# The delta net's substitution on 128 partitions, four columns of a block in each

## The chip, the cores and the metric

The kernel runs on one core of a Trainium2 chip. The metric is the device time of one execution in microseconds (us). The core's engines take their instructions from queues of their own, each in order: TensorE (PE; PEld is its weight load), VectorE (DVE), ScalarE (ACT), GpSimd (POOL) and SyncE (SP), which issues nearly all DMAs of this kernel.

## The reference

One layer of a hybrid decoder on 512 tokens with a width of 2048: six heads of stick-breaking attention, four groups of a gated short convolution, six heads of a gated delta net, an output projection, an MLP with squared ReLU, and the norms. The change is in the delta net. It cuts the 512 tokens into chunks and solves a unit lower triangular system in each:

```python
m = jnp.where(strict, jnp.einsum('bhnid,bhnjd->bhnij', k_beta, k) * decay, 0.0)
eye = jnp.eye(C, dtype=f32)
t_mat = lax.linalg.triangular_solve(eye + m, jnp.broadcast_to(eye, m.shape),
                                    left_side=True, lower=True, unit_diagonal=True)
u = t_mat @ v_beta
w = t_mat @ (k_beta * jnp.exp(g)[..., None])
...
def step(state, xs):
    q_c, k_c, u_c, w_c, a_c, gl_c = xs
    v_new = u_c - w_c @ state
    o = q_c @ state + a_c @ v_new
    state = state * jnp.exp(gl_c)[..., None, None] + jnp.swapaxes(k_c, -1, -2) @ v_new
    return state, o
```

## The kernel before

All large products are made as three matmuls of fp32r halves (`mm3`, L109 to L111). A weight arrives as `raw` by a DMA that SP issues (L100), ACT rounds it to `whi` (L103), DVE makes the rest `wlo` (L104); both feed PE. `gemm` makes 48 such matmuls of 512 columns from four weight loads of 256 KB. There are four buffers each of `raw`, `whi` and `wlo`, and three PSUM banks for results.

The delta net takes chunks of 128 tokens, four per head (NB = 4). For each head `gdn_in` makes three projections, their convolutions, SiLU and norms (DVE and ACT), and from them `MT`, the strictly triangular matrices of the four chunks, 128 x (4 x 128) fp32. `gdn_base` inverts unit triangular matrices: first the four 32 x 32 blocks on the diagonal of each chunk, 16 blocks per head, by substitution on DVE; then the blocks off the diagonal by small matmuls (L452, L461, L471, L476, L482; PSUM tiles `b`), which put the inverse back into `MT`. `gdn_scan` runs the chunks of a head in order (PSUM tiles `s` and `o`). `sc_group` and `gdn_gate` are other products of the same stage, without a tie to the substitution; they are written between the heads' parts.

Before the change the substitution goes like this. SP writes `MT` whole to DRAM (`sm`, L424); four DMAs fetch the diagonal blocks, one for each group of 32 rows, so that each of 16 partitions holds one whole block of 32 x 32 (`Bq`, L426). `Yq` is cleared and given a diagonal of ones by POOL (L431, L432). For i = 31 to 1, DVE multiplies a column of the block with a row of `Yq` (L436, i x (32 - i) products on each partition) and subtracts that from `Yq` (L438). `Yq` goes to DRAM (`sy`, L440) and back by four DMAs (L443) into `Xc`, 32 rows by row group; DVE turns its 32 x 32 blocks into `X0` (L447), which L452 takes first. `Bq` and `Yq` have two halves for odd and even heads.

A planner lays out the order of each engine's instructions ahead of the run, with a cost model of its own (`TileContext(nc, schedule_with_timeline_sim=True)`). `base` and `scan` put the head's substitution and scan 2000 places ahead in its priorities, weight loads go 400 ahead. The program's order of the heads' parts is that of L654 to L680: gdn_in(0), base(0), gdn_in(1), scan(0), sc_group(0), base(1), gdn_in(2), and so on.

Of the kernel before, what the change touches and what calls it, by code (L numbers as in the profile page):

```python
# [11 lines left out]
F32 = mybir.dt.float32  # L12
F32R = mybir.dt.float32r
AF = mybir.ActivationFunctionType
ALU = mybir.AluOpType

P = 128
T = 512
NB = T // P
# [35 lines left out]
def trunk(ctx, tc, xT, wv1, wv2, wa, wo, wu, wd, vec, wf, out, dbg=None):  # L55
    nc = tc.nc
    V, S, G, PE = nc.vector, nc.scalar, nc.gpsimd, nc.tensor
# [9 lines left out]
    dr = ctx.enter_context(tc.tile_pool(name="dr", bufs=1, space=bass.MemoryType.DRAM))  # L67
# [9 lines left out]
    def xps(tag):  # L77
        pool, bufs = pool_of[tag]
        return pool.tile([P, 512], F32, name=tag, tag=tag, bufs=bufs)
# [8 lines left out]
    def tmp(n=512):  # L88
        return per.tile([P, n], F32, name="tmp", tag="tmp", bufs=4)

    def big():
        return big_pool.tile([P, 2, 512], F32R, name="big", tag="big", bufs=16, align_bytes=256)

    def f32t(shape, name):
        return per.tile(shape, F32, name=name)
# [26 lines left out]
    def gemm(src, acts):  # L122
        p = mmps()
        for c in range(KT // CHUNK_KT):
            gemm_chunk(p, src, acts, c)
        return p
# [27 lines left out]
    ident = f32t([P, P], "ident")  # L154
# [32 lines left out]
    for k in range(KT):  # L187
# [3 lines left out]
        a = big()  # L191
# [4 lines left out]
        for b in range(NB):  # L196
            s = slice(b * P, (b + 1) * P)
# [15 lines left out]
    p = xps("r")  # L213
# [3 lines left out]
    p = xps("r")  # L217
# [24 lines left out]
    for c in range(2):  # L242
        t = tmp()
# [35 lines left out]
    def ytile(i):  # L279
        return y_pool.tile([P, 512], F32, name="y", tag=f"y{i}", bufs=(10, 6)[i])  # L280
# [27 lines left out]
    p = xps("r")  # L308
# [20 lines left out]
    def gt(shape, name, tag=None, bufs=1, dt=F32):  # L329
        return gp.tile(shape, dt, name=name, tag=tag or name, bufs=bufs)  # L330

    q4 = lambda a: a.rearrange("p (b f) -> p b f", b=NB)
# [25 lines left out]
    heads, gb = {}, {}  # L358

    def gdn_in(h):  # L360
# [29 lines left out]
        for b in range(NB):  # L390
            S.activation(out=q4(dts)[:, b], in_=q4(dts)[:, b], func=AF.Copy, scale=be[:, b, h:h + 1])
        AT, MT = ytile(1), gt([P, 512], "MT", bufs=3)
        for c in range(2):
# [4 lines left out]
            s = slice(2 * c, 2 * c + 2)  # L398
            V.tensor_tensor(out=q4(MT)[:, s], in0=pv[:, :, 0], in1=q4(dts)[:, s], op=ALU.mult)
            V.tensor_tensor(out=q4(AT)[:, s], in0=pv[:, :, 1], in1=q4(dti)[:, s], op=ALU.mult)  # L400
        st.update(kq=kq, vtok=vtok, AT=AT, MT=MT)
        heads[h] = st
# [10 lines left out]
    def gdn_base(h):  # L413


        MT = heads[h]["MT"]
        if not gb:
            gb.update(Bq=gt([P, 32, 32], "Bq"), Yq=gt([P, 32, 32], "Yq"), tq=gt([P, 256], "tq"),
                      Xc=gt([P, 256], "Xc"))
            G.memset(gb["Xc"], 0.0)  # L420
        Bq, Yq, tq, Xc = (gb[n] for n in ("Bq", "Yq", "tq", "Xc"))
        p0 = 32 * (h % 2)
        sm = dr.tile([P, NB, P], F32, name="sm", tag="sm", bufs=2)
        nc.sync.dma_start(out=sm, in_=q4(MT))  # L424
        for s in range(NB):
            nc.sync.dma_start(  # L426
                out=Bq[p0 + 4 * s:p0 + 4 * s + 4],
                in_=sm[32 * s:32 * s + 32, :, 32 * s:32 * s + 32].rearrange("a k b -> k a b"))
        B, Y, t = Bq[p0:p0 + 16], Yq[p0:p0 + 16], tq[p0:p0 + 16]
        Yf = Y.rearrange("p a b -> p (a b)")  # L430
        G.memset(Yf, 0.0)  # L431
        G.memset(Yf[:, 0:1024:33], 1.0)  # L432
        for i in range(31, 0, -1):
            n = 32 - i
            tv = t[:, :i * n].rearrange("p (a b) -> p a b", a=i)
            V.tensor_tensor(out=tv, in0=B[:, 0:i, i:i + 1].broadcast_to([16, i, n]),  # L436
                            in1=Y[:, i:i + 1, i:32].broadcast_to([16, i, n]), op=ALU.mult)
            V.tensor_tensor(out=Y[:, 0:i, i:32], in0=Y[:, 0:i, i:32], in1=tv, op=ALU.subtract)  # L438
        sy = dr.tile([16, 32, 32], F32, name="sy", tag="sy", bufs=2)
        nc.sync.dma_start(out=sy, in_=Y)  # L440
        Xv = q4(Xc)
        for s in range(NB):
            nc.sync.dma_start(  # L443
                out=Xv[32 * s:32 * s + 32, :, 32 * (s % 2):32 * (s % 2) + 32],
                in_=sy[4 * s:4 * s + 4].rearrange("k a b -> a k b"))
        X0 = gt([P, 256], "X0")
        V.transpose(out=X0, in_=Xc)  # L447
        p = xps("b")
        pv = q4(p[:, :128])
        for b in range(NB):  # L450
            for s in (0, 64):
                PE.matmul(pv[s + 32:s + 64, b], lhsT=q4(MT)[s:s + 32, b, s + 32:s + 64],  # L452
                          rhs=q4(X0)[s:s + 32, b, 0:32], start=True, stop=True)
        A1 = gt([P, 128], "A1")
        S.copy(out=A1[32:64], in_=p[32:64, :128])
        V.tensor_copy(out=A1[96:128], in_=p[96:128, :128])
        p = xps("b")
        pv = q4(p[:, :128])
        for b in range(NB):
            for s in (32, 96):  # L460
                PE.matmul(pv[s - 32:s, b], lhsT=q4(A1)[s:s + 32, b], rhs=Xv[s:s + 32, b, 32:64], start=True, stop=True)  # L461
        for s in (0, 2):
            r = slice(32 * s, 32 * s + 32)
            if s:
                V.tensor_scalar(out=Xv[r, :, 32:64], in0=pv[r], scalar1=-1.0, scalar2=None, op0=ALU.mult)
            else:
                S.mul(out=Xv[r, :, 32:64], in_=pv[r], mul=-1.0)
        lo, hi = slice(0, 64), slice(64, P)
        p = xps("b")
        for b in range(NB):  # L470
            PE.transpose(p[lo, b * 64:b * 64 + 64], Xc[lo, b * 64:b * 64 + 64], ident[lo, lo])  # L471
        X1 = gt([P, 256], "X1")
        S.copy(out=X1[lo], in_=p[lo, :256])
        p = xps("b")
        for b in range(NB):
            PE.matmul(q4(p[:, :256])[hi, b], lhsT=q4(MT)[lo, b, hi], rhs=q4(X1)[lo, b], start=True, stop=True)  # L476
        S.copy(out=X1[hi], in_=p[hi, :256])
        for r in (lo, hi):
            V.tensor_copy(out=q4(MT)[r, :, r], in_=Xv[r])
        p = xps("b")  # L480
        for b in range(NB):
            PE.matmul(q4(p[:, :256])[lo, b], lhsT=q4(X1)[hi, b], rhs=Xv[hi, b], start=True, stop=True)  # L482
        S.mul(out=q4(MT)[lo, :, hi], in_=q4(p[:, :256])[lo], mul=-1.0)
# [161 lines left out]
    def base(h):  # L645
        with tc.high_priority(CPRIO):
            gdn_base(h)
# [72 lines left out]
    for k in ORDER:  # L720
        a = big()
# [46 lines left out]
    for m in range(KT):  # L768
# [5 lines left out]
        p = gemm(wo[m], yh)  # L774
# [12 lines left out]
        i = m // 2  # L787
        half_split(XP[i][:, m % 2:m % 2 + 1], y[:, :HT].unsqueeze(1))
        if m % 2:
            t = late.tile([P, 4, HT], F32, name="xsum", tag="xsum", bufs=2)  # L790
# [387 lines left out]
```

## Time and profile before

| what | value |
|---|---|
| median of 3 runs | 2188.25 us (2186.37 to 2189.2) |
| the profiled execution | 2187.66 us |
| its span | 2185.7 us |
| PE busy | 2145.4 us, 98% |
| DVE busy | 1710.6 us, 78% |
| ACT busy | 1069.7 us, 49% |
| mean granted clock of TensorE | 0.994 of full |

The profile is of one execution. Its span runs from the first instruction to the last; the device time of that execution is 2.0 us longer. Times in the rows below count from the start of the span. A mean granted clock of 1.00 is 2.4 GHz; the other level is 1.2 GHz.

### The profile page before, as it was taken

To read this page: it belongs to the slowest core of one execution; us is meant where nothing else is said; L and a number is where in the kernel's file an instruction comes from. 1 tells how busy PE (TensorE), PEld (TensorE's weight loads), DVE (VectorE), ACT (ScalarE), POOL (GpSimd) and SP (SyncE) were. 2 spreads that over 40 slices of the span, in tenths; PEclk is the share of its full clock that TensorE was granted. 3 is DMA by queue.
4 is the path that set the end of the run, shared out by engine and by line. 5 is a ranking of instruction groups with operands and counts; after the bars stand their busy time and mean duration, and the time that the engine had idled before them with its cause. 6 is when DMAs were issued, how large, how long until landed. Compare 5 with 4: busy or idle time off the path is not lost.

```text
span 2185.7 us, 33120 instructions
## 1 busy us (share of the span) xinstructions
PE 2145.4 (98%) x12674; PEld 1885.9 (86%) x12674; DVE 1710.6 (78%) x2348; ACT 1069.7 (49%) x1622; POOL 142.8 (7%) x197
## 2 busy tenths in 40 slices
PE   9999999999999999999999999999899999999997
PEld 8887787787989888799999999999778888888886
DVE  6689899744656755587888788877888898899887
ACT  6745566333434544454454445454444454445454
POOL 0000000000000011100000000000001000000102
PEclk9999999999999999999999999999999999999999
DMA  6332222222222254656666666666987877787764
GB/s 191 99 97 84 76 79 86 81 80 97 78 83 83 86 164 149 212 175 196 196 176 176 200 196 178 173 200 193 289 278 180 243 221 202 199 234 215 184 199 115
DMA packets 157822, 352.16 MB, mean 161 GB/s; under 512 B 19840, under 2 KB 59904, under 8 KB 157536
## 3 DMA queue, kind: packets, MB, share of 16 engines
q1 hardware_dynamic: 143552, 299.19, 40.5%
q0 software_dynamic: 13824, 50.34, 13.3%
q8 instruction: 99, 1.62, 0.3%
q14 instruction: 59, 0.48, 0.1%
q10 hardware_dynamic: 288, 0.52, 0.1%
HBM read 304.51 MB, written 45.48 MB: 160 GB/s over the span
## 4 chain that ended last, share of the span: by engine, by line
PE 87%; DVE 6%; DMA 2%; ACT 2%; issue 1%; SPq 0%; DVEq 0%; ACTq 0%
PE pu L111 10%; PE pu L110 10%; PE pu L109 10%; PE mm L109 9%; PE mm L110 9%; PE mm L111 9%; PE pp L110 9%; PE pp L109 9%; PE pp L111 9%; DVE wlo L104 1%; DVE Yq L438 1%; DVE tq L436 1%; PE mm L273 1%; PE mm L274 1%; PE mm L272 1%
## 5 line engine op out<-in xcount | busy, mean ns | idle before, releaser
L824 ACT CAST W<-q 128x1024 fp32r<-128x1024 f32 x446 | 465.4, 1051 | 573.2 <-PE pp L111 259.8
L825 DVE TENSOR_TENSOR W<-q,W 128x1024 fp32r<-128x1024 f32 x446 | 542.7, 1225 | 126.8 <-ACT W L824 122.6
L109 PE MATMUL mm<-big,whi 128*128 128x512 f32 x1024 | 406.1, 397 | 2.0 <-DVE tmp L557 1.6
L111 PE MATMUL mm<-big,wlo 128*128 128x512 f32 x1024 | 405.1, 396 | 0.0
L110 PE MATMUL mm<-big,whi 128*128 128x512 f32 x1024 | 404.5, 395 | 0.0
L109 PE MATMUL pp<-W,A 128*128 128x512 f32 x896 | 348.1, 391 | 8.9 <-DVE xq L989 5.3
L110 PE MATMUL pp<-W,A 128*128 128x512 f32 x896 | 349.9, 391 | 2.6 <-DVE W L825 2.6
L111 PE MATMUL pp<-W,A 128*128 128x512 f32 x896 | 349.4, 390 | 1.1 <-DVE A L825 1.1
L104 DVE TENSOR_TENSOR wlo<-raw,whi 128x512 fp32r<-128x512 f32 (+1 forms) x292 | 196.8, 675 | 149.3 <-ACT whi L103 135.5
L103 ACT CAST whi<-raw 128x512 fp32r<-128x512 f32 (+1 forms) x292 | 176.5, 605 | 271.7 <-PE mm L110 232.9
L109 PE MATMUL pu<-XS,W 128*128 128x256 f32 x1024 | 287.9, 281 | 1.1 <-ACT W L824 0.8
L111 PE MATMUL pu<-XS,W 128*128 128x256 f32 x1024 | 287.5, 281 | 0.8 <-DVE W L825 0.8
L110 PE MATMUL pu<-XS,W 128*128 128x256 f32 x1024 | 287.6, 281 | 0.0
L109 PEld LDWEIGHTS mm<-big,whi 128*128 128x128 f32 x1024 | 193.4, 189 | 41.1 <-DVE tmp L557 1.8
L111 PEld LDWEIGHTS mm<-big,wlo 128*128 128x128 f32 x1024 | 193.3, 189 | 40.1 <-DVE wlo L104 0.5
L110 PEld LDWEIGHTS mm<-big,whi 128*128 128x128 f32 x1024 | 193.3, 189 | 39.1 <-DVE big L723 0.3
L109 PEld LDWEIGHTS pp<-W,A 128*128 128x128 f32 x896 | 168.6, 188 | 45.9 <-DVE xq L989 5.7
L110 PEld LDWEIGHTS pp<-W,A 128*128 128x128 f32 x896 | 168.6, 188 | 38.7 <-DVE W L825 3.9
L111 PEld LDWEIGHTS pp<-W,A 128*128 128x128 f32 x896 | 168.5, 188 | 36.7 <-DVE A L825 1.8
L842 DVE TENSOR_TENSOR q<-q 128x1024 f32<-128x1024 f32 x160 | 196.2, 1227 | 1.5
L109 PEld LDWEIGHTS pu<-XS,W 128*128 128x128 f32 x1024 | 193.6, 189 | 2.1 <-ACT W L824 1.7
L111 PEld LDWEIGHTS pu<-XS,W 128*128 128x128 f32 x1024 | 193.4, 189 | 1.0 <-DVE W L825 1.0
(291 smaller groups left out, 3305.8 us busy)
## 6 DMA issues: line engine op xcount, KB each, us to landing
q<-in_wu_dram SPq DMA_DIRECT2D x128, 512.0 KB
q<-in_wd_dram SPq DMA_DIRECT2D x128, 512.0 KB
raw<-in_wa_dram SPq DMA_DIRECT2D x192, 256.0 KB
hs<-h SPq DMA_DIRECT2D x32, 1024.0 KB
q<-in_wd_dram POOLq DMA_DIRECT2D x64, 512.0 KB, 7.5
ha<-hs SPq DMA_DIRECT2D x55, 512.0 KB
raw<-in_wo_dram SPq DMA_DIRECT2D x64, 256.0 KB
q<-in_wu_dram POOLq DMA_DIRECT2D x32, 512.0 KB, 5.4
```

The source lines that it names most:

```text
L103: S.copy(out=hi[:, :n], in_=raw[:, :n])
L104: V.tensor_tensor(out=lo[:, :n], in0=raw[:, :n], in1=hi[:, :n].bitcast(F32), op=ALU.subtract)
L109: PE.matmul(p, lhsT=lh, rhs=rh, start=first, stop=False, skip_group_check=more)
L110: PE.matmul(p, lhsT=lh, rhs=rl, start=False, stop=False, skip_group_check=more)
L111: PE.matmul(p, lhsT=ll, rhs=rh, start=False, stop=last, skip_group_check=more)
L272: PE.matmul(o, lhsT=xw[k][:, 0, s], rhs=hi[:, ws], start=k == 0 and b % 2 == 0, stop=False)
L273: PE.matmul(o, lhsT=xw[k][:, 0, s], rhs=lo[:, ws], start=False, stop=False)
L274: PE.matmul(o, lhsT=xw[k][:, 1, s], rhs=hi[:, ws], start=False, stop=k == KT - 1 and b % 2 == 1)
L436: V.tensor_tensor(out=tv, in0=B[:, 0:i, i:i + 1].broadcast_to([16, i, n]), in1=Y[:, i:i + 1, i:32].broadcast_to([16, i, n]), op=ALU.mult)
L824: S.copy(out=o[:, 0], in_=src)
L825: V.tensor_tensor(out=o[:, 1], in0=src, in1=o[:, 0].bitcast(F32), op=ALU.subtract)
L842: on_v = lambda t, u: V.tensor_tensor(out=t, in0=t, in1=u, op=ALU.add)
```

## The change

The 16 blocks of a head are spread over all 128 partitions: partition 8k + g holds the whole block k and four columns (c = 4g to 4g + 3) of its inverse. Four DMAs write only the diagonal blocks to DRAM, into `sm` of 16 x 32 x 32; one DMA fetches them, with each block repeated for eight partitions, into `B`. `Y` holds the inverse by columns, 4 x 32 on each partition, and starts as a copy of `id`, which is the identity cut in the same way; `id` is made once, by a trip of the identity through DRAM (`one`). A step multiplies the column i of the block (its elements are 128 bytes apart), repeated for four columns of the inverse, with the element i of each of these columns, 4i products on each partition, and subtracts. `Y` has the other index inside, so the DMAs now fill `X0` and the transpose writes `Xc`. All that follows is as before. The two instructions of a step are still a multiply and a subtraction, and there are still 31 steps.

```diff
--- before.py
+++ after.py
@@ -413,38 +413,42 @@
     def gdn_base(h):
...
         MT = heads[h]["MT"]
         if not gb:
-            gb.update(Bq=gt([P, 32, 32], "Bq"), Yq=gt([P, 32, 32], "Yq"), tq=gt([P, 256], "tq"),
-                      Xc=gt([P, 256], "Xc"))
-            G.memset(gb["Xc"], 0.0)
-        Bq, Yq, tq, Xc = (gb[n] for n in ("Bq", "Yq", "tq", "Xc"))
-        p0 = 32 * (h % 2)
-        sm = dr.tile([P, NB, P], F32, name="sm", tag="sm", bufs=2)
-        nc.sync.dma_start(out=sm, in_=q4(MT))
+            gb.update(X0=gt([P, 256], "X0"), Xc=gt([P, 256], "Xc"), id=gt([P, 4, 32], "id"))
+            G.memset(gb["X0"], 0.0)
+            one = dr.tile([32, 32], F32, name="one")
+            nc.sync.dma_start(out=one, in_=ident[:32, :32])
+            one = one.rearrange("(g c) a -> g (c a)", g=8)
+            nc.sync.dma_start(out=gb["id"].rearrange("p c a -> p (c a)"),
+                              in_=one.unsqueeze(0).broadcast_to([16, 8, 128]))
+        X0, Xc = gb["X0"], gb["Xc"]
+        sm = dr.tile([16, 32, 32], F32, name="sm", tag="sm", bufs=2)
         for s in range(NB):
-            nc.sync.dma_start(
-                out=Bq[p0 + 4 * s:p0 + 4 * s + 4],
-                in_=sm[32 * s:32 * s + 32, :, 32 * s:32 * s + 32].rearrange("a k b -> k a b"))
-        B, Y, t = Bq[p0:p0 + 16], Yq[p0:p0 + 16], tq[p0:p0 + 16]
-        Yf = Y.rearrange("p a b -> p (a b)")
-        G.memset(Yf, 0.0)
-        G.memset(Yf[:, 0:1024:33], 1.0)
+            nc.sync.dma_start(out=sm[4 * s:4 * s + 4].rearrange("k a b -> a k b"),
+                              in_=q4(MT)[32 * s:32 * s + 32, :, 32 * s:32 * s + 32])
+        B = gt([P, 32, 32], "Bq", bufs=2)
+        nc.sync.dma_start(out=B.rearrange("p a b -> p (a b)"),
+                          in_=sm.rearrange("k a b -> k (a b)").unsqueeze(1).broadcast_to([16, 8, 1024]))
+        Y = gt([P, 4, 32], "Yq", bufs=2)
+        t = gt([P, 128], "tq")
+        G.tensor_copy(out=Y, in_=gb["id"])
         for i in range(31, 0, -1):
-            n = 32 - i
-            tv = t[:, :i * n].rearrange("p (a b) -> p a b", a=i)
-            V.tensor_tensor(out=tv, in0=B[:, 0:i, i:i + 1].broadcast_to([16, i, n]),
-                            in1=Y[:, i:i + 1, i:32].broadcast_to([16, i, n]), op=ALU.mult)
-            V.tensor_tensor(out=Y[:, 0:i, i:32], in0=Y[:, 0:i, i:32], in1=tv, op=ALU.subtract)
+            tv = t[:, :4 * i].rearrange("p (c a) -> p c a", c=4)
+            V.tensor_tensor(out=tv, in0=B[:, 0:i, i].unsqueeze(1).broadcast_to([P, 4, i]),
+                            in1=Y[:, :, i:i + 1].broadcast_to([P, 4, i]), op=ALU.mult)
+            V.tensor_tensor(out=Y[:, :, 0:i], in0=Y[:, :, 0:i], in1=tv, op=ALU.subtract)
         sy = dr.tile([16, 32, 32], F32, name="sy", tag="sy", bufs=2)
-        nc.sync.dma_start(out=sy, in_=Y)
+        nc.sync.dma_start(out=sy.rearrange("k c a -> (k c a)").rearrange("(p f) -> p f", p=P),
+                          in_=Y.rearrange("p c a -> p (c a)"))
         Xv = q4(Xc)
         for s in range(NB):
             nc.sync.dma_start(
-                out=Xv[32 * s:32 * s + 32, :, 32 * (s % 2):32 * (s % 2) + 32],
-                in_=sy[4 * s:4 * s + 4].rearrange("k a b -> a k b"))
-        X0 = gt([P, 256], "X0")
-        V.transpose(out=X0, in_=Xc)
+                out=q4(X0)[32 * s:32 * s + 32, :, 32 * (s % 2):32 * (s % 2) + 32],
+                in_=sy[4 * s:4 * s + 4].rearrange("k c a -> c k a"))
+        V.transpose(out=Xc, in_=X0)
```

## Rows read from the trace of the kernel before

**Rows 1.** The page, part 1: busy us, share of the span, instructions.

```profile
PE 2145.4 (98%) x12674; PEld 1885.9 (86%) x12674; DVE 1710.6 (78%) x2348; ACT 1069.7 (49%) x1622; POOL 142.8 (7%) x197
```

**Rows 2.** The chain that ended last, summed by line, with its shares of the span.

```profile
by line: PE pu L111 9.6%; PE pu L110 9.6%; PE pu L109 9.5%; PE mm L109 8.9%; PE mm L110 8.9%; PE mm L111 8.9%; PE pp L110 8.6%; PE pp L109 8.5%; PE pp L111 8.5%; issue 1.3%; DVE wlo L104 0.9%; DVE Yq L438 0.8%; DVE tq L436 0.7%; PE mm L273 
```

**Rows 3.** Windows: length, busy us (instructions) of each engine, granted clock, DMA share, GB/s.

```profile
0.00:25.00 25.00, 23.07 (x136) 20.59 (x137) 19.53 (x38) 22.19 (x43) 3.66 (x14) 1.00 0.83 269
64.00:500.00 436.00, 423.73 (x2168) 343.51 (x2168) 360.13 (x796) 232.32 (x489) 16.45 (x42) 0.98 0.27 85
...
260.00:280.00 20.00, 18.09 (x108) 14.20 (x109) 17.33 (x31) 13.44 (x31) 1.70 (x4) 0.74 0.09 28
400.00:420.00 20.00, 18.23 (x110) 14.15 (x109) 14.28 (x40) 4.83 (x11) 0.00 (x0) 0.91 0.29 92
```

**Rows 4.** PE's waits, 100 to 500 us: releaser, us in total, times, longest.

```profile
PE b L452 <- DVE X L447: 2.9, 3, 1.4
PE s L501 <- DVE bp L498: 1.8, 1, 1.8
PE mm L109 <- DVE tmp L557: 1.6, 1, 1.6
PE i L354 <- ACT g L350: 1.3, 1, 1.3
```

**Rows 5.** Groups of DVE, 64 to 500 us: busy us, mean ns, idle us before them.

```profile
L104 DVE TENSOR_TENSOR wlo<-raw,whi 128x512 fp32r<-128x512 f32 x126 | 86.7, 688 | 26.0 <-ACT whi L103 17.4 <-ACT X L477 2.7 <-PE s L501 2.6
L438 DVE TENSOR_TENSOR Yq<-Yq,tq 16x60 f32<-16x60 f32 (+15 forms) x186 | 62.8, 338 | 4.9
L436 DVE TENSOR_TENSOR tq<-Bq,Yq 16x60 f32<-16x60 f32 (+15 forms) x186 | 62.7, 337 | 11.4 <-DMA Bq<-sm 6.8
```

**Rows 6.** Groups of DVE by form, 100 to 500 us, columns as above.

```profile
L438 DVE TENSOR_TENSOR Yq<-Yq,tq 16x240 f32<-16x240 f32 x12 | 4.7, 394 | 0.2
...
L438 DVE TENSOR_TENSOR Yq<-Yq,tq 16x112 f32<-16x112 f32 x12 | 3.1, 262 | 0.3
```

**Rows 7.** Timeline: start us, us; first step of one head, last of another.

```profile
116.86 0.20 DVE L436 TENSOR_TENSOR tq<-Bq,Yq 16x31 f32<-16x31 f32 x1 [0.75 <-DMA Bq<-sm]
...
253.25 0.18 DVE L436 TENSOR_TENSOR tq<-Bq,Yq 16x31 f32<-16x31 f32 x1
```

**Rows 8.** DMA issues: times, KB each, median us to landing.

```profile
q<-in_wu_dram POOLq DMA_DIRECT2D x32, 512.0 KB, 5.4
...
sm<-MT SPq DMA_DIRECT2D x6, 256.0 KB
```

**Rows 9.** Pieces of the chain that ended last: start us, us.

```profile
283.61 2.00 DMA sm<-MT
...
291.97 2.36 DMA raw<-in_wa_dram
...
399.02 3.53 DMA sm<-MT
403.68 2.14 DMA Bq<-sm
```

**Rows 10.** Timeline of SP's queue around 402 us.

```profile
402.57 1.47 SPq L426 DMA_DIRECT2D Bq<-sm  x4
```

**Rows 11.** Timeline of POOL at the start.

```profile
3.34 0.29 POOL L170 TENSOR_SCALAR_AFFINE_SELECT U<-ones 128x128 f32<-128x128 f32 x1
```

**Rows 12.** Timeline of SP's queue at the start.

```profile
4.08 0.43 SPq L100 DMA_DIRECT2D raw<-in_wv_dram  x1
```

**Rows 13.** Timeline of all engines, 404 to 413 us.

```profile
405.94 0.20 DVE L436 TENSOR_TENSOR tq<-Bq,Yq 16x31 f32<-16x31 f32 x1 [4.10 <-DMA Bq<-sm]
...
411.97 0.80 PE L501 MATMUL s<-bp,MT 128*128 128x128 f32 x2 [1.77 <-DVE bp L498]
```

## The prediction, made before the change was run

> **What bounds the kernel now.** The page comes first: TensorE (PE) is busy for 98% of the span, VectorE (DVE) for 78% [rows 1]. Then the chain that ended last: it names the two substitution lines (L436, L438) with 0.7% and 0.8% of 2185.7 us, 33 us together [rows 2]. Read alone, the chain would promise a third of these 33 us. It doesn't say whether PE had other work meanwhile, so the stage itself is looked at next. The delta net runs from 64 to 500 us. In those 436 us PE is busy 423.7 and idle 12.3; DVE is busy 360.1 (83%) [rows 3]. PE is the bound here too, with DVE close behind. PE's granted clock is 1.00 in most of the stage; the stretch 260 to 280 us has 0.74 (part of it at 1.2 instead of 2.4 GHz) and 400 to 420 us has 0.91 [rows 3]. At full clock these stretches would have given 20 x 0.26 = 5.2 and 20 x 0.09 = 1.8 us more of PE. So the change can win at most about 12.3 + 5.2 + 1.8 = 19 us, 0.9%, however much DVE it frees: the rest of the stage is matmuls that nobody removes. PE's own waits say who holds it: the longest is the first matmul behind the substitution (L452, for the transpose of L447), then work of the scan and of a convolution group that sits in DVE's queue [rows 4]. The four shown are 7.6 us; the three that end in DVE are 6.3.
>
> **DVE's part.** The substitution has 62 instructions per head, 372 in six heads, both before and after. Before, they took 62.8 + 62.7 = 125.5 us, 337 ns each, beside 86.7 us for the splitting of weights (L104), which feeds the matmuls from the same in-order queue [rows 5]. Before, an instruction has i(32-i) elements on each of 16 partitions, up to 256; now it has 4i on each of 128, at most 124. The mean of 4i for i = 31..1 is 64. Price per element, from two forms of the same line: (394 - 262)/(240 - 112) = 1.03 ns, and 262 - 112 x 1.03 = 147 ns without elements [rows 6]. Partitions don't enter: L104 with 512 elements on all 128 partitions takes 688 ns [rows 5], and the line gives 147 + 528 = 675. So 372 x (147 + 64 x 1.03) = 372 x 213 = 79 us.
>
> The new multiply reads a column of B, one element each 128 bytes. The old one did so at its first step (i = 31, one column left), and read contiguously at its last (i = 1); both have 31 elements. They took 0.20 and 0.18 us [rows 7]: 20 ns for 31 elements, 0.65 ns each. That puts 64 x 0.65 = 42 ns on 186 instructions, 7.8 us. I take it, since the old first step is the same read: 87 us. The saving is 125.5 - 87 = 38.5 us, 6.4 us per head; the bounds are 46.5 us (no price for the stride) and 125.5 - 372 x 0.262 = 28 us (every instruction as dear as the one with 112 elements).
>
> The Trainium skill (SBUF — State Buffer, section "Door 1: The DMA port swizzle") speaks against this read: accesses that cross to another 16-byte line pay a penalty, so four fp32 is as far as one can step for free. It has no figure; the 20 ns per 31 elements agree with it in sign. By the rule the new total is the 87 us, without it the 79 us.
>
> **The transfers.** Before, one DMA writes MT whole (256 KB), four of 16 KB fetch the diagonal blocks [rows 8]. In the chain the write took 2.00 to 3.53 us, the last fetch 2.14, a 256 KB weight load 2.36 [rows 9]. SP issues four such DMAs in 1.47 us [rows 10], so three in front of the last one are 1.1 us. Old way at its quickest: 2.0 + 1.1 + 2.1 = 5.2 us. Now four DMAs write only the blocks, in runs of 128 bytes, and one fetch brings 128 rows of 4 KB, 512 KB where 64 KB went. No row shows such a write or a replicated read. The write is bounded by 2.0 and 3.5 us; I take 2.1, that of the fetch with the same runs. The read is bounded below by the 256 KB load (2.4 us) and above by the 512 KB load that POOL issues in a later stage (5.4 us [rows 8]). I take 2.4 plus 1.0 for another 256 KB at the 269 GB/s of the first 25 us [rows 3], 3.4 us, as queue and issuer are those of the weight load. New way: 1.1 + 2.1 + 3.4 = 6.6 us, bounds 5.5 and 10.0; so 1.4 us later per head, against 6.4 us that DVE gives back behind it. SP waits for the write to land as before, and queued behind that wait are the weight loads, as before. They now share the DMA engines with 64 + 512 KB per head in place of 256 + 64, 256 KB more; the engines' busy share is 0.27 in this stage [rows 3], so I cost that at nothing. If the cover by loads made ahead is gone, it costs up to 256 KB at 269 GB/s, 1.0 us per head.
>
> **Small parts.** POOL's two memsets per head become one copy of 128x128, priced like POOL's select of that shape, 0.29 us [rows 11]; POOL is busy 16 of 436 us [rows 3], so either way it is hidden. The identity is sent out and fetched once: two issues on SP, whose queue is full at the start at 0.43 us each [rows 12], and a landing of some 2 us between them. Hidden if the planner puts loads between; 2 us if the wait stands in front of weight loads. I take 1. Swapping which buffer the DMA fills and which the transpose writes moves a reuse wait from a DMA onto DVE; the readers it waits for (L479, L482 of the head before) stand in front of that head's scan in the order of the program, so I take nothing; without that cover DVE would wait once per head, at most for the like of the 4.10 us that it has waited for a transfer [rows 13].
>
> **The sum.** Of the 6.3 us of PE waits that end in DVE I let two thirds go, 4: the substitution ends sooner and the scan's small steps no longer queue between so many substitution steps, but the wait of L452 also has the landing of sy in it, which stays. The clock's 5.2 us go with the waits that stand before and in that stretch: PE is idle 1.4 us from 240 to 260 us and 1.9 from 260 to 280 [rows 3]; the 1.8 us I leave. With 1 us for the start: -4 - 5.2 + 1 = -8.2. The profiled execution took 2187.66 us (span 2185.7 and 2.0 around it), 0.6 below the median of the runs shown; 2187.7 - 8.2 = 2179.5, say 2180 us.
>
> **Rivals.** *Hidden anyway.* PE is 97% busy in the stage and the planner lays out a new order for every engine: the 38.5 us that DVE gains are idle time of DVE, and PE's waits turn up at other places, with a like sum and a like dip of the clock. For it: every instruction order here comes from the planner, and L452's wait ends in a transfer that doesn't change. Against it: 6.3 of the 7.6 us above end in DVE. Time 2184 to 2192, centre 2187. *The block lands late.* DVE runs in order; a first multiply that waits for B holds the weight splits behind it. It has happened once: at 405.94 us DVE had waited 4.10 us for Bq, and at 411.97 PE waited 1.77 us for a scan step that DVE had got to late [rows 13], with the dip of 1.8 us. At the upper bound of 10 us B is 4.8 us later than in the old way at its quickest, as much as that wait. If three or four of six heads meet it, it is 3.5 x (1.8 + 1.8) = 12.6 us, less what the shorter substitution still gives back (some 4 us): 2196. It decides from a landing some 4 us later than the planner expects. *The full prize.* All 19 us: 2169. It would need the planner to cover every wait, but one of the four longest ends in ACT and the longest has a transfer in it.
>
> For the second rival the Trainium skill (DMA: Bandwidth & Descriptors, section "Specifications") has a rule: below 512 bytes a DMA does read-modify-write, and the new write goes to DRAM in runs of 128. No run here shows such a write; the chances stand without it.
>
> **Chances.** Gain beyond 4.4 us (0.2%, about what a measurement of this kernel can tell from no change): 0.56, nearly all of it the forecast, 0.04 the full prize. Hidden anyway, within 4.4 us: 0.27. Late block, slower by more: 0.17. The range reaches from near the full prize to where half of the late block's cases lie above: 2171 to 2193. The likeliest case alone is 2174 to 2183.
>
> **What the profile after would show.** L436 and L438 at 372 instructions, 80 to 90 us, the multiply some 40 ns dearer than the subtraction; DVE in the stage near 320 us; no first multiply that waits over 4 us for Bq; the fetch of B landing in 2.4 to 5.4 us; PE idle in 64 to 500 us near 8 us and no stretch of clock 0.74. I am wrong if PE's idle time stays at 12 us with DVE 40 us lighter (hidden), or if DVE's waits for Bq, 6.8 us now [rows 5], grow by 10 or more (late block).

## The result, and the profile after

The changed kernel takes 2175.02 us (median of 4 runs, 2174.82 to 2176.32), the kernel before 2188.23. The ratio is 0.9939, with a 95% interval of 0.9924 to 0.9955: 13.2 us faster. The forecast was 2180.

The page of the changed kernel, part 1, and the first line of its part 4 (the chain that ended last, by engine), beside [rows 1]:

```profile
PE 2143.5 (99%) x12674; PEld 1885.9 (87%) x12674; DVE 1663.8 (77%) x2348; ACT 1070.9 (49%) x1622; POOL 140.0 (6%) x191
...
PE 94%; DMA 2%; DVE 2%; ACT 1%; issue 1%; SPq 0%; ACTq 0%; DVEq 0%
```

PE has the same work in 12.6 us less span. DVE is 47 us less busy. The chain that ended last spends 2% on DVE, where before its two substitution lines alone had 1.5% [rows 2].

Windows of the changed kernel, columns as in [rows 3]:

```profile
0.00:25.00 25.00, 22.11 (x121) 19.76 (x122) 18.06 (x34) 20.35 (x39) 2.88 (x12) 1.00 0.80 258
64.00:500.00 436.00, 434.86 (x2249) 353.97 (x2248) 319.22 (x805) 237.04 (x497) 13.44 (x38) 1.00 0.30 92
240.00:260.00 20.00, 20.00 (x111) 16.36 (x110) 18.72 (x43) 15.84 (x34) 0.83 (x4) 1.00 0.29 89
260.00:280.00 20.00, 20.00 (x114) 16.07 (x113) 13.48 (x31) 11.92 (x27) 1.27 (x3) 1.00 0.32 84
400.00:420.00 20.00, 20.00 (x108) 16.24 (x108) 14.09 (x43) 9.34 (x20) 0.00 (x0) 1.00 0.31 93
```

PE's idle time from 64 to 500 us is 436 - 434.9 = 1.1 us, where it was 12.3 [rows 3]; the clock of 0.74 and 0.91 is 1.00. The window of 240 to 260 us in the kernel before, which the prediction draws on, has this row:

```profile
240.00:260.00 20.00, 18.60 (x103) 15.42 (x104) 14.78 (x41) 6.62 (x14) 1.09 (x2) 1.00 0.28 86
```

PE's waits, 64 to 500 us, of the changed kernel (releaser, us, times, longest), against [rows 4]:

```profile
PE r L219 <- ACT R L139: 0.8, 1, 0.8
PE mm L109 <- DVE xp L337: 0.2, 1, 0.2
```

This is all that is listed: no wait on the substitution, the scan or a convolution is left, and the first one stands at the head of the stage.

DVE's groups, 64 to 500 us, of the changed kernel, columns as in [rows 5] (L440 is the multiply, L442 the subtraction):

```profile
L104 DVE TENSOR_TENSOR wlo<-raw,whi 128x512 fp32r<-128x512 f32 x131 | 90.2, 689 | 40.3 <-ACT whi L103 35.5 <-PE mm L110 2.1 <-PE s L505 2.0
L440 DVE TENSOR_TENSOR tq<-Bq,Yq 128x124 f32<-128x124 f32 (+30 forms) x186 | 50.4, 271 | 18.4 <-DMA Bq<-sm 14.6
L442 DVE TENSOR_TENSOR Yq<-Yq,tq 128x124 f32<-128x124 f32 (+30 forms) x186 | 42.0, 226 | 3.6
```

The two lines take 92.4 us, where it was 125.5, and the multiply is 45 ns dearer than the subtraction. DVE waits longer for the block than before, 14.6 against 6.8 us; nobody on PE pays for it. The timeline of the first head shows how late the block is. SP's queue, then DVE:

```profile
113.18 1.76 SPq L430 DMA_DIRECT2D sm<-MT  x4
116.19 0.56 SPq L433 DMA_DIRECT2D Bq<-sm  x1
```

```profile
121.69 0.38 DVE L440 TENSOR_TENSOR tq<-Bq,Yq 128x124 f32<-128x124 f32 x1 [2.68 <-DMA Bq<-sm]
```

The fetch goes out at 116.2 us and the first multiply starts at 121.7, having waited 2.68 us for it.

Where the stage begins and ends is read from two groups, the sum of squares (first matmul of L214) and the first scores of the attention (tile z). First the kernel before, then the changed one; the times behind the durations are the first and the last start:

```profile
L214 PE MATMUL r<-acc,ones x2: 592/592/592, 63.2 to 63.7; 128*128 128x512 f32 x2
```

```profile
L109 PE MATMUL z<-sk,sq x18: 278/338/496, 544.3 to 723.2; 128*128 128x512 f32 x6, 128*128 128x384 f32 x6, 128*128 128x256 f32 x6
```

```profile
L214 PE MATMUL r<-acc,ones x2: 592/592/592, 65.4 to 65.8; 128*128 128x512 f32 x2
```

```profile
L109 PE MATMUL z<-sk,sq x18: 278/338/497, 527.4 to 706.8; 128*128 128x512 f32 x6, 128*128 128x384 f32 x6, 128*128 128x256 f32 x6
```

The stage lasts from 63.2 to 544.3, 481.1 us, before, and from 65.4 to 527.4, 462.0 us, after. So it wins 19.1 us, more than the whole execution does. The windows of just this stage, first before, then after:

```profile
63.20:544.30 481.10, 467.10 (x2370) 378.86 (x2368) 375.48 (x822) 246.69 (x517) 16.45 (x42) 0.99 0.27 86
65.40:527.40 462.00, 460.51 (x2370) 374.97 (x2368) 328.58 (x821) 246.21 (x516) 13.44 (x38) 1.00 0.30 92
```

PE's idle time falls by 12.5 us (14.0 to 1.5) and its busy time, with as many matmuls, by 6.6. Together that is the 19.1. DVE is 46.9 us less busy, more than the 33.1 that the two lines lose. The durations of DVE's instructions in the stage add up to 34.1 us less; the other 12.8 us are overlap, as an instruction of DVE can start in the trace before the one ahead of it has ended, and in the changed kernel more of that time overlaps.

The start loses 2.2. The first matmul of the down projection starts at 1551.3 before and at 1538.8 after, so what lies between the first scores and it takes 1007.0 and 1011.4 us: 4.4 are given back there. The rest is equal within 0.1. Sum: 2.2 - 19.1 + 4.4 - 0.1 = -12.6, the difference of the spans. These are the parts of one execution of each kernel.

Some of the 4.4 is clock. About the same 40 us of the two kernels, behind the attention:

```profile
910.00:950.00 40.00, 36.41 (x281) 34.75 (x280) 31.95 (x39) 22.44 (x32) 3.33 (x3) 0.96 0.71 227
```

```profile
894.00:934.00 40.00, 34.90 (x250) 33.07 (x251) 29.29 (x37) 20.26 (x30) 3.34 (x3) 0.91 0.72 240
```

40 x (0.96 - 0.91) = 2.0 us. The other 2.4 are spread over small waits and were not traced further.

### The profile page after: what moved, and what is told of

It reads as the page before. It is cut to its first block, busy times and chain, and to the rows that moved or that the text cites. A ratio compares the mean times of both kernels' runs of the same rounds, so it can differ in the third digit from the quotient of the medians.

```text
span 2173.1 us, 33090 instructions
## 1 busy us (share of the span) xinstructions
PE 2143.5 (99%) x12674; PEld 1885.9 (87%) x12674; DVE 1663.8 (77%) x2348; ACT 1070.9 (49%) x1622; POOL 140.0 (6%) x191
## 4 chain that ended last, share of the span: by engine, by line
PE 94%; DMA 2%; DVE 2%; ACT 1%; issue 1%; SPq 0%; ACTq 0%; DVEq 0%
PE mm L110 11%; PE mm L109 11%; PE mm L111 11%; PE pu L109 10%; PE pu L111 10%; PE pu L110 10%; PE pp L110 9%; PE pp L109 9%; PE pp L111 9%; PE mm L273 1%; PE mm L274 1%; PE mm L272 1%; DMA xq<-xs 1%; DMA tmp<-x 1%; PE i L397 1%
```

## The experiments

Lengths of the stage are worked out for each run as above, from L214's first matmul to the first of tile z. Each ratio is to executions of the kernel before that were made in the same round.

| run | median, us | ratio to before (interval) | stage, us | PE idle, 64 to 500 us |
|---|---|---|---|---|
| before | 2188.2 | | 481.1 | 12.3 |
| after | 2175.0 | 0.9939 (0.9924 to 0.9955) | 462.0 | 1.1 |
| old_fewer | 2173.5 | 0.9929 (0.9913 to 0.9945) | 465.5 | 5.6 |
| wide | 2180.6 | 0.9961 (0.9946 to 0.9976) | 466.8 | 3.7 |
| id_late | 2170.7 | 0.9916 (0.9899 to 0.9932) | 462.1 | 1.1 |
| old_plan | 2187.1 | 0.9998 (0.9989 to 1.0008) | 480.0 | 12.5 |
| old_swap | 2204.2 | 1.0076 (1.0059 to 1.0092) | 496.3 | 21.5 |
| old_blocks | 2179.6 | 0.9965 (0.9952 to 0.9978) | 472.7 | 10.0 |
| rowread | 2174.2 | 0.9941 (0.9926 to 0.9956) | 462.0 | 1.1 |
| new_plan | 2175.7 | 0.9947 (0.9932 to 0.9961) | 462.4 | 1.2 |
| swap_row | 2188.0 | 0.9998 (0.9988 to 1.0007) | 480.9 | 11.0 |
| blocks_plan | 2181.9 | 0.9970 (0.9958 to 0.9983) | 474.7 | 9.5 |
| blocks_four | 2186.1 | 0.9991 (0.9982 to 1.0001) | 476.3 | 9.7 |
| fetch_twice | 2183.8 | 0.9983 (0.9974 to 0.9992) | 472.7 | 9.1 |

The theory at this point: the time that DVE is given back removes PE's waits. Its rivals: the transfers and buffers do it, or it is the luck of one plan among many.

**DVE's time alone, with the old layout (old_fewer).**

```diff
         for i in range(31, 0, -1):
+            if 13 <= i <= 18:
+                continue
             n = 32 - i
```

> The old substitution with the six middle steps (i = 13 to 18) left out, so the inverse is not complete; transfers and buffers as before. This takes some 12 x 0.40 x 6 = 29 us from DVE, nearly as much as the change (33 us). If the time that DVE is given back makes the gain, PE's idle time from 64 to 500 us falls to a few us and the time is 2175 to 2180 us. If the gain is from the new transfers and buffers, it stays at 2185 to 2191.

DVE's two lines, 64 to 500 us:

```profile
L440 DVE TENSOR_TENSOR Yq<-Yq,tq 16x31 f32<-16x31 f32 (+12 forms) x150 | 47.0, 313 | 4.0
L438 DVE TENSOR_TENSOR tq<-Bq,Yq 16x31 f32<-16x31 f32 (+12 forms) x150 | 46.9, 313 | 13.2 <-DMA Bq<-sm 9.4
```

They take 93.9 us, within 1.5 of the changed kernel's 92.4, with every transfer and buffer as before. The stage wins 15.6 us and the whole 15.2, a little more than was expected. So with less time on DVE and the old transfers most of the gain is there. The planner gave this kernel an order of its own, though, and the run alone can't tell the order from DVE's time.

**DVE's time put back, with the new layout (wide).**

```diff
-        Y = gt([P, 4, 32], "Yq", bufs=2)
-        t = gt([P, 128], "tq")
+        Y8 = gt([P, 8, 32], "Yq", bufs=2)
+        Y = Y8[:, 0:4]
+        t = gt([P, 256], "tq")
         G.tensor_copy(out=Y, in_=gb["id"])
+        G.tensor_copy(out=Y8[:, 4:8], in_=gb["id"])
...
-            tv = t[:, :4 * i].rearrange("p (c a) -> p c a", c=4)
+            tv = t[:, :8 * i].rearrange("p (c a) -> p c a", c=8)
```

> The new kernel with eight columns on each partition in place of four, the other four a copy of the first that nobody reads: each step is twice as long, the transfers are the same, and one more copy on POOL per head. DVE's two lines should take 115 to 125 us, as before the change. If the time that DVE is given back makes the gain, it is lost: 2185 to 2191 us. If transfers and buffers make it, 2173 to 2178.

```profile
L442 DVE TENSOR_TENSOR tq<-Bq,Yq 128x248 f32<-128x248 f32 (+30 forms) x186 | 73.0, 392 | 19.0 <-DMA Bq<-sm 15.5
L444 DVE TENSOR_TENSOR Yq<-Yq,tq 128x248 f32<-128x248 f32 (+30 forms) x186 | 55.0, 295 | 3.7
```

128.0 us, 2.5 more than before the change and 3 more than expected. Neither time came: 5.6 of the 13.2 us are lost, the rest stays. In the stage 4.8 of 19.1 are lost. But the run doesn't put all of DVE's time back. The stages of old_fewer and of wide:

```profile
63.30:528.80 465.50, 459.92 (x2370) 375.37 (x2369) 345.59 (x752) 248.39 (x521) 16.24 (x42) 1.00 0.28 88
65.20:532.00 466.80, 461.44 (x2369) 375.25 (x2367) 361.29 (x822) 245.74 (x517) 15.59 (x42) 1.00 0.30 91
```

In wide DVE is busy for 361.3 us of the stage, 14.2 less than before the change: its two lines are longer, but more of the time of DVE's instructions overlaps. So the 14.3 us of stage that stay are not shown to come from something other than DVE; the new transfers and a new order are in this run as well. The gains of old_fewer and wide, 15.6 + 14.3 against 19.1, don't add up in any case, because PE's idle time and lost clock are all there is to win.

**Luck of the plan (old_plan, new_plan).** Both change one number in both kernels:

```diff
-WPRIO = 400
+WPRIO = 380
```

> The kernel before with weight loads 380 in place of 400 places ahead in the planner's priorities, nothing else. It shows what another plan alone is worth. If DVE's time decides, the time stays at 2185 to 2191 us with PE idle 9 to 15 us from 64 to 500 us. If the gain is the luck of a new plan, a change of 5 us or more to either side is as likely.

> The new kernel with weight loads 380 in place of 400 places ahead in the planner's priorities, nothing else. If the gain stands on the new mechanism and not on one lucky plan, 2171 to 2179 us with PE idle at most 4 us from 64 to 500 us; if on luck, above 2182.

Both stay where their parents are. But neither is another plan. Put in the order of their starts, by tiles, operation and shape, the 2348 instructions of DVE and the 12674 matmuls of PE are the same in old_plan as in the kernel before, and the same in new_plan as in the changed kernel. So these runs repeat their parents and say nothing on the luck of a plan. As a repeat, old_plan shows the stretch of half clock of the kernel before once more (window of 240 to 280 us):

```profile
240.00:280.00 40.00, 36.14 (x204) 28.87 (x203) 31.47 (x71) 19.43 (x43) 1.78 (x5) 0.87 0.19 59
```

So it is not the accident of one execution. The repeats also show how far a stage scatters without any change of order: 481.1 and 480.0 us here, 462.0 and 462.4 in the changed kernel. What other orders do is seen in swap_row and old_blocks, below.

**The swap alone (old_swap, swap_row).** Y's indices are exchanged on the 16 partitions, the DMAs fill X0, the transpose writes Xc:

```diff
-            V.tensor_tensor(out=tv, in0=B[:, 0:i, i:i + 1].broadcast_to([16, i, n]),
-                            in1=Y[:, i:i + 1, i:32].broadcast_to([16, i, n]), op=ALU.mult)
-            V.tensor_tensor(out=Y[:, 0:i, i:32], in0=Y[:, 0:i, i:32], in1=tv, op=ALU.subtract)
+            V.tensor_tensor(out=tv, in0=B[:, 0:i, i].unsqueeze(1).broadcast_to([16, n, i]),
+                            in1=Y[:, i:32, i:i + 1].broadcast_to([16, n, i]), op=ALU.mult)
+            V.tensor_tensor(out=Y[:, i:32, 0:i], in0=Y[:, i:32, 0:i], in1=tv, op=ALU.subtract)
```

> The kernel before with the swap alone: Y with its indices exchanged on the old 16 partitions (the same i(32-i) elements per instruction), so that the DMAs fill X0, which L452 reads, and the transpose writes Xc. Transfers and DVE's time as before (about 125 us). In the run with the double width DVE's time was that of before and three quarters of the stage's gain stayed. If the swap makes that part, since L452 no longer waits for a transpose in DVE's queue, the time falls to 2174 to 2182 us. If the swap does nothing, as the prediction had it, 2185 to 2191.

```profile
L436 DVE TENSOR_TENSOR tq<-Bq,Yq 16x60 f32<-16x60 f32 (+15 forms) x186 | 87.3, 470 | 9.6 <-DMA Bq<-sm 4.9
...
L438 DVE TENSOR_TENSOR Yq<-Yq,tq 16x60 f32<-16x60 f32 (+15 forms) x186 | 62.0, 333 | 4.7
```

It was not the swap alone. Now each element of the multiply is read 128 bytes from the last one, and the multiply takes 470 ns where it took 337 [rows 5]; the two lines take 24 us more together. The time rises by 16.5 us: the same lever as in old_fewer, turned the other way. So swap_row takes the stride out.

```diff
-                            in0=B[:, 0:i, i].unsqueeze(1).broadcast_to([16, n, i]),
+                            in0=B[:, i, 0:i].unsqueeze(1).broadcast_to([16, n, i]),
```

> The kernel before with the swap alone, as in old_swap, but the multiply reads row i of the block, which is contiguous, so it does not compute the inverse. old_swap could not tell the swap from the 25 us that the 128-byte steps put on DVE; here DVE's two lines should be at 124 to 127 us, as before. If the swap helps by itself, 2176 to 2184 us. If it does nothing, 2185 to 2191. If L452's wait for the transfer (10.2 us in old_swap) is the swap's own cost, above 2191.

The two lines are at 124.8 us, the time is 2188.0: the swap by itself does nothing.

The pair shows two things more. swap_row has a different order from the kernel before: at most 620 of DVE's 822 instructions of the stage stand in the same sequence. The stage takes 480.9 us in place of 481.1, so in this one case a new order with the swap is worth nothing. And old_swap has the order of swap_row throughout, on DVE and on PE, so these two differ by the stride alone. Their stages, first swap_row, then old_swap:

```profile
63.50:544.40 480.90, 469.88 (x2365) 380.29 (x2364) 376.57 (x824) 246.81 (x520) 16.85 (x42) 0.98 0.27 85
63.30:559.60 496.30, 471.90 (x2365) 378.51 (x2364) 399.36 (x824) 245.76 (x520) 16.76 (x42) 0.98 0.26 82
```

With the order and the transfers unchanged, 22.8 us more on DVE make the stage 15.4 us longer, 13.4 of it idle time of PE. This is the plainest sign that PE's waits follow DVE's time.

**The transfers in front of the substitution (old_blocks, blocks_plan, blocks_four).** The old substitution, with the blocks alone written and one fetch of 64 KB; the same with the other planner number; the same with four fetches.

```diff
-        sm = dr.tile([P, NB, P], F32, name="sm", tag="sm", bufs=2)
-        nc.sync.dma_start(out=sm, in_=q4(MT))
+        sm = dr.tile([16, 32, 32], F32, name="sm", tag="sm", bufs=2)
         for s in range(NB):
-            nc.sync.dma_start(
-                out=Bq[p0 + 4 * s:p0 + 4 * s + 4],
-                in_=sm[32 * s:32 * s + 32, :, 32 * s:32 * s + 32].rearrange("a k b -> k a b"))
+            nc.sync.dma_start(out=sm[4 * s:4 * s + 4].rearrange("k a b -> a k b"),
+                              in_=q4(MT)[32 * s:32 * s + 32, :, 32 * s:32 * s + 32])
+        nc.sync.dma_start(out=Bq[p0:p0 + 16], in_=sm)
```

> The kernel before with the transfers in front of the substitution changed alone: four DMAs write only the diagonal blocks, one fetches them (64 KB, not replicated). If the order of these transfers makes part of the gain, the time falls below 2184 us. If not, 2185 to 2191 us.

> old_blocks with weight loads 380 in place of 400 places ahead. If its 8 us are from the transfers, they stay: 2177 to 2182 us, and no stretch of half clock from 64 to 500 us. If they were one lucky plan, 2184 to 2191 us, or another value altogether.

In blocks_four the last line is, in place of the single fetch:

```diff
+        for s in range(NB):
+            nc.sync.dma_start(out=Bq[p0 + 4 * s:p0 + 4 * s + 4], in_=sm[4 * s:4 * s + 4])
```

> old_blocks with four fetches of 16 KB, in place of one of 64 KB: only the write differs from the kernel before. If the smaller write (64 in place of 256 KB) makes the 8 us, 2177 to 2182 us. If the single fetch makes it, 2185 to 2191 us.

The windows of 240 to 280 us, first old_blocks, then blocks_four:

```profile
240.00:280.00 40.00, 39.30 (x218) 31.77 (x218) 35.99 (x78) 23.04 (x48) 3.01 (x7) 1.00 0.25 77
```

```profile
240.00:280.00 40.00, 36.95 (x210) 29.82 (x210) 32.51 (x72) 20.42 (x46) 2.99 (x6) 0.87 0.19 58
```

old_blocks is 8.1 us faster than the kernel before, blocks_plan 6.4, with DVE's two lines at 124.3 us. blocks_four is 2.1 us faster, with an interval that reaches 1. In the stage the three win 8.4, 6.4 and 4.8 us. blocks_plan has the order of old_blocks and is a repeat of it, not a second plan; the half clock that its expectation excluded is there, at another place:

```profile
480.00:500.00 20.00, 16.98 (x74) 13.74 (x74) 13.71 (x24) 7.12 (x17) 0.10 (x1) 0.83 0.22 71
```

blocks_four has the order of the kernel before on DVE and PE, so the 4.8 us of its stage are the smaller write's: PE is idle for 9.7 in place of 12.3 us, and the dip at 400 to 420 us (0.91 in [rows 3]) is gone:

```profile
400.00:420.00 20.00, 20.00 (x131) 15.84 (x130) 16.04 (x44) 5.77 (x13) 0.00 (x0) 1.00 0.26 84
```

In this execution 2.7 us of it are given back behind the stage. The 3.6 us of stage between blocks_four and old_blocks (1.6 in the repeat) can't be put down to the single fetch: the planner made another order for it (at most 584 of DVE's 822 instructions stand in the same sequence), and the two executions of the one order are 2.0 apart themselves. What the windows show is the clock, 1.00 against 0.87, at a PE idle time that is nearly the same (10.0 and 9.7 us from 64 to 500 us), only less of it in one place (0.7 and 3.1 us of these 40).

**The stride (rowread).**

```diff
-            V.tensor_tensor(out=tv, in0=B[:, 0:i, i].unsqueeze(1).broadcast_to([P, 4, i]),
+            V.tensor_tensor(out=tv, in0=B[:, i, 0:i].unsqueeze(1).broadcast_to([P, 4, i]),
```

> The new kernel with the multiply reading row i of the block, which is contiguous, in place of column i; so it does not compute the inverse. All else is as in the new kernel. If the 128-byte steps are the reason that the multiply takes 271 ns and the subtraction 226, the multiply falls to 225 to 235 ns and DVE's two lines to 84 to 86 us. The time should stay within 2 us of 2175, since PE no longer waits in this stage.

```profile
L442 DVE TENSOR_TENSOR Yq<-Yq,tq 128x124 f32<-128x124 f32 (+30 forms) x186 | 41.8, 225 | 3.6
L440 DVE TENSOR_TENSOR tq<-Bq,Yq 128x124 f32<-128x124 f32 (+30 forms) x186 | 41.7, 224 | 17.6 <-DMA Bq<-sm 13.8
```

The multiply falls from 271 to 224 ns, level with the subtraction. 47 ns for 64 elements is 0.73 ns each. The whole doesn't follow: with PE idle for 1.1 us, 9 us less on DVE win nothing. The order is that of the changed kernel, so nothing else differs.

**A late block (fetch_twice).** The fetch of B is issued twice; the second waits for the first to land.

> The new kernel with the fetch of B issued twice in a row, 1 MB in place of 512 KB per head, so that B lands some 3 us later. If a late block costs PE time, as the second rival had it, 6 heads with 1 to 3 us each: 2181 us or more, with DVE's waits for Bq above 25 us. If PE is covered by then, within 3 us of 2175.

The two fetches of the first head, 5.6 us apart:

```profile
116.57 0.56 SPq L434 DMA_DIRECT2D Bq<-sm  x1
122.16 0.53 SPq L434 DMA_DIRECT2D Bq<-sm  x1
```

DVE's waits for the block and PE's longest wait, 64 to 500 us:

```profile
DVE tq L441 <- DMA Bq<-sm: 29.0, 6, 6.3
```

```profile
PE b L457 <- DMA X<-sy: 4.1, 1, 4.1
```

Twice the wait of the changed kernel (14.6 us), and 8.8 of the 13.2 us are gone, with PE idle for 9.1 us. Nearly half of that is one wait of the first matmul behind the substitution, which a late block makes late. So a late block can cost PE. The run also holds SP's queue behind the first fetch and has an order of its own, so not all of the loss is shown to be the block's. In id_late DVE waits 17.1 us for the block and PE is idle for 1.1, so by these two runs the cost begins somewhere between 17.1 and 29.0 us of such waits.

**The identity's trip (id_late).** The start of the changed kernel holds it in front of weight loads (SP's queue):

```profile
2.20 0.43 SPq L423 DMA_DIRECT2D one<-ident  x1
2.67 0.43 SPq L190 DMA_DIRECT2D xr<-in_xT_dram  x1
3.14 0.43 SPq L100 DMA_DIRECT2D raw<-in_wv_dram  x1
4.83 0.64 SPq L425 DMA_DIRECT2D id<-one  x1
```

SP stands still from 3.57 to 4.83 us, 1.2 of it waiting for the write of `one` to land.

```diff
     gdn_in(0)
+    gdn_setup()
     base(0)
```

(`gdn_setup` has the lines of `if not gb:`.)

> The new kernel with the trip of the identity (one, id) and the clearing of X0 in the program's order behind gdn_in(0) and without the raised priority. If the 2.1 us that the start up to 64 us got longer by come from these two DMAs in front of the weight loads, the time falls by 1.5 to 2.5 us to about 2173. If the start only fell otherwise in the plan, it stays within 0.5 us of 2175.

The stage starts at 63.9 in place of 65.4 us: 1.5 back, as expected. The median is 4.3 below that of the changed kernel, more than expected, though the two intervals overlap by 0.0008. The other 3 us lie between the scores and the down projection, where PE's clock doesn't fall in the first 40 us:

```profile
893.00:933.00 40.00, 35.35 (x281) 33.56 (x282) 31.05 (x39) 21.60 (x31) 3.34 (x3) 1.00 0.66 213
```

DVE and PE have the same order there as in the changed kernel, so this part is not a new plan's; why the clock stays up is open. This is the fastest version of all that ran.

## Why the prediction was right

**The bound.** From 64 to 500 us the kernel before had 12.3 us of idle PE and 7.0 us of lost clock to give, 19 us at most. The stage gave 19.1. That the two are so near is partly luck, as the stage in fact runs to 544 us and had 14.0 us of idle time; but the four kernels with next to no PE waits in it (after, rowread, new_plan and id_late, all of one order) end at 462.0 to 462.4 us, and 9 us less on DVE move that by nothing. The reading of the bound was the step that carried the forecast.

**The sum, where it was mis-sized.** The prediction let 4 us of PE's waits go and 5.2 of the clock's 7.0. Measured: 11.2 us of waits, 7.0 of clock. The term that was too small is "Of the 6.3 us of PE waits that end in DVE I let two thirds go"; it held back the wait of L452 for the landing in it, and it left out the waits that end in ACT and the short ones that [rows 4] doesn't list. In the changed kernel next to none of them is left. That PE's waits follow DVE's time is shown by old_swap beside swap_row, and old_fewer agrees. That each head's block now comes earlier against PE's other matmuls, so that these cover it, is the likely way; no run shows it by itself. So the case that had 0.04, the full prize, came in the stage; 6.6 us were given back, 2.2 at the start and 4.4 behind the stage, which the sum had at 1.

**DVE's price.** 87 us forecast, 92.4 measured. The stride was priced at 42 ns per multiply and is 45 to 47. That is near partly by luck: the old last step (i = 1), which the prediction takes for a contiguous read, reads one element of the block 31 times. Too low was the price of an instruction without it: 226 ns where the line gave 213, 13 ns on 372 instructions, 4.8 us. The line came from instructions of 112 elements and more, and the new ones have 64 in the mean. DVE's busy time in the stage still came out as forecast, near 320 us (319.2 from 64 to 500 us), but for a reason that the sum doesn't have, the greater overlap. The rule of the Trainium skill (SBUF — State Buffer, section "Door 1: The DMA port swizzle") that a step beyond 16 bytes costs holds here: the multiply on 128-byte steps is dearer than the subtraction in every run that has them (50.4 against 42.0 us in the changed kernel), and level in rowread and swap_row.

**The transfers.** The block was to land 3.4 us after its issue, within 2.4 to 5.4; in the first head the multiply starts 5.5 us after it, and over the six heads the landing takes 4.9 us in the median. So it is the price of a 512 KB load and not the weight load's that fits. Landings, first two rows of the changed kernel, then one of old_blocks:

```profile
q<-in_wu_dram SPq DMA_DIRECT2D x128, 512.0 KB, 4.5
Bq<-sm SPq DMA_DIRECT2D x6, 512.0 KB, 4.9
```

```profile
Bq<-sm SPq DMA_DIRECT2D x6, 64.0 KB, 2.3
```

From the write to the first multiply are 121.7 - 113.2 = 8.5 us, forecast 6.6. The four writes in runs of 128 bytes are not the reason: from their first issue to that of the fetch are 116.19 - 113.18 = 3.0 us, where the forecast had 1.1 + 2.1 = 3.2. The Trainium skill (DMA: Bandwidth & Descriptors, section "Specifications") says that below 512 bytes a DMA does read-modify-write; no run here writes the same bytes in longer runs, so what that costs in these writes is not shown. DVE's waits for it grew by 7.8 us; the prediction's sign of trouble was 10. Its second rival described a mechanism that fits fetch_twice; the changed kernel lies short of the point where it decides.

**Hidden anyway.** It did not come: PE's waits did not turn up at other places of the stage, where 1.5 us of idle time are left. Behind it 4.4 us were given back, 2.0 of them clock.

**Small parts.** The swap does nothing by itself, as taken. The start costs 2.2 where 1 was taken and 2 was the bound; id_late gets 1.5 of that back.

**What stays open.** How the 19.1 us divide between DVE's time, the transfers and the order that the planner made is not settled. DVE's time alone, at a fixed order, is shown only in the dearer direction (old_swap beside swap_row); the smaller write alone, at a fixed order, wins 4.8 us of stage (blocks_four). The changed kernel, old_fewer, wide, old_blocks and fetch_twice each have an order of their own. One new order with the old DVE time and the old transfers in front was run, swap_row, and it won 0.2 us; one is too few to rule out that other orders are luckier. Whether one fetch wins more than four is open too (3.6 us of stage in old_blocks, 1.6 in its repeat): DVE waits longer for the block there (8.1 against 2.8 us), and what is seen is only that PE's idle time is less bunched and the clock stays up.

## What to carry to other kernels

When an engine at 83% feeds one at 97%, the prize is the idle time and lost clock of the second one, counted in that stage, and not the time that the first one is given back; but most of that prize can come for a part of it, and more DVE savings behind that (rowread) are worth nothing. Before a run is taken for another plan, compare the order of the instructions in the two traces: a changed planner number gave the same order here. Count setup work that a high priority drags to the start of the program: two small DMAs in front of the weight loads cost as much as a tenth of the gain. Price a transfer that replicates data by the bytes that it writes: 64 KB fetched once landed in 2.3 us, the same 64 KB fetched eight times over in 4.9 us, near the 4.5 us of a plain load of 512 KB.

## What the runs showed of the hardware that was not expected

Reading fp32 at 128-byte steps costs a two-input DVE operation about 0.75 ns more per element: 47 ns for 64 elements (after against rowread), and 135 ns for 176 (old_swap against swap_row, 470 and 335 ns, with the mean of i(32 - i) being 176). Against the 1.03 ns per element that [rows 6] give, that is some 70% more.

With nearly the same idle time of PE from 64 to 500 us (9.7 and 10.0 us), the clock fell to 1.2 GHz for part of the stretch from 240 to 280 us in blocks_four (0.87 in the mean), where PE was idle for 3.1 us of the 40, and stayed at 2.4 GHz in old_blocks (1.00), where it was idle for 0.7.

DVE's busy time and the durations of its instructions are not the same sum: in the stage of the changed kernel the durations add up to 365.2 us and DVE is busy for 328.6, before the change to 399.3 and 375.5. A saving read from durations alone misses 12.8 us here. One such overlap in the first head of the changed kernel, where the second instruction starts 0.09 us before the first ends:

```profile
122.10 0.29 DVE L442 TENSOR_TENSOR Yq<-Yq,tq 128x124 f32<-128x124 f32 x1
122.30 0.68 DVE L351 TENSOR_TENSOR g<-g 128x512 fp32r<-128x512 f32 x1
```
